# Selection scores of one block summed by ScalarE and GpSimd, its top-k rounds put last

## The chip, the cores and the metric

The kernel runs on 1 core of one Trainium2 chip. The metric is the time of one execution in microseconds (us), the median of several runs. The engines are TensorE (PE in the profile; its weight loads are PEld), VectorE (DVE), ScalarE (ACT), GpSimd (POOL) and SyncE (SP, which issues the transfers here). Each runs its own list of instructions in order and waits on the others by semaphores.

## The reference

A two-layer encoder for 512 frames of width 1024: layer one has sparse attention ("mixer A"), layer two latent attention, each followed by a squared-ReLU MLP. The change lies in mixer A, where a small indexer picks 128 keys for every query:

```python
logits = jnp.einsum('bthd,bsd->bths', qib, ki)          # 8 indexer heads
score = jnp.einsum('bths,bth->bts', jax.nn.relu(logits), wib)
score = jnp.where(visible[None], score, -jnp.inf)       # chunks of 64 frames
_, sel = lax.top_k(score, top_k)                        # top_k = 128
...
s = jnp.einsum('btgrd,btkgd->btgrk', qg, kg) * scale    # only the selected keys
p = jax.nn.softmax(s, axis=-1)
o = jnp.einsum('btgrk,btkgd->btgrd', p, vg)
```

The kernel doesn't gather keys: it makes a mask per query that is 0 for a selected key and a large negative number for the others, and adds it to all scores of the attention.

## The kernel before, in words

The 512 queries are four blocks of 128, numbered `qb` 0 to 3. Block 0 sees at most 128 keys, so it needs no selection. Block `qb` has `N = (qb + 1) * 128` key columns; "the second block" is `qb` 1 (256 columns), the third `qb` 2 (384), the fourth `qb` 3 (512).

Every product in float32 quality is made of three matmuls (`mm3`, L227 to L229) from a high and a low part of each operand. `Weights.convert` makes these parts: a cast on ACT (`w.._hi`, L143) and a subtraction on POOL (`w.._lo`, L150), five weight tiles ahead; a tile's buffer comes free when PE has used it.

In mixer A the order of the work is this:

- Projection of the indexer's rows (`ip`), with rotary embedding on DVE, the last for `inat[0]` (L390 to L393).
- `proj_tiles` is the projection of keys and values: 32 steps of three matmuls into the PSUM tiles `pp`, taken one at a time by `next(side)`, so that PE has work between other things.
- `q_turn` (L802) transposes the indexer's queries into `qip`, L811 its keys into `kip`; copies on ACT and differences on DVE give `qis` and `ki`.
- The score loop (L846): for each block and each of 8 heads one projection step, two matmuls `lp` (L852, L853; PSUM banks 0 and 1 in turn), for head 0 a relu and scaling on DVE (L856), for the others a relu on ACT (L859, tile `relu`) and `relu * weight + sum` on DVE (L860) into `acc[qb]`, which the trace calls `bias`.
- The selection, `rounds(qb)`: 16 rounds for each block, each a MAX8 (L829, the eight largest) and a MATCH_REPLACE8 (L831, which overwrites them with `TAKEN`; its first part shows as MATCH_VALUE_LOAD). Then L833 turns the block into its mask. `turns()` takes the blocks that are ready in rotation. Steps of it are drawn in the score loop and in the 64 steps of the query projection that follow (L927).
- Attention by head (`plan_heads`): scores `s_ps` on PE (L559), `top` on DVE, which adds the mask (L567; `smask` for block 0), exponential on ACT (L572), transposes (L578) and their parts, products with the values (L621), and the output projection `wo_ps` as a filler.

In the score loop PE's instructions keep the order in which they are written (`manual_schedule`), though later work may be put between them; a scheduler orders the other engines' lists, and PE's elsewhere, when the program is built. So a change in one place of mixer A gives new lists for all of it.

Of the kernel before, what the change touches and what calls it, by code (L numbers as in the profile page):

```python
# [11 lines left out]
F32 = mybir.dt.float32  # L12
F32R = mybir.dt.float32r
I32 = mybir.dt.int32
AF = mybir.ActivationFunctionType
OP = mybir.AluOpType
PSUM = bass.MemoryType.PSUM

P = 128
D = 1024  # L20
S = 512
NT = S // P
KD = D // P
CHUNK = 64
# [7 lines left out]
IDX_HEADS = 8  # L32
# [10 lines left out]

DFF = 4096
NEG = -1.0e30
FILL = -3.0e38
TAKEN = -3.4e38


RAWS = 3  # L50
# [154 lines left out]
def trunk(ctx: ExitStack, tc: tile.TileContext, x, positions, attn_norm, mlp_norm, a_w_in, a_w_out,  # L205
          b_w_in, b_q_norm, b_kv_norm, b_w_q_up, b_w_kv_up, b_w_out, mlp_w_up, mlp_w_down,
          final_norm, out):
    nc = tc.nc
# [17 lines left out]
    def mm3(ps, lh, ll, rh, rl, first, last):  # L226
        nc.tensor.matmul(ps, lh, rh, start=first, stop=False)  # L227
        nc.tensor.matmul(ps, lh, rl, start=False, stop=False)  # L228
        nc.tensor.matmul(ps, ll, rh, start=False, stop=last)  # L229
# [5 lines left out]

    lead = const.tile([P, 72], F32, name="lead")
    nc.gpsimd.memset(lead, 0.0)
    table = const.tile([P, 2], F32, name="table")
    nc.scalar.activation(table[:, 0:1], ones, AF.Sin)

# [271 lines left out]
    def run(gen):  # L512
        for _ in gen:
            pass
# [183 lines left out]
    def mixer_a():  # L698
        with ExitStack() as sa:
# [4 lines left out]
            bias = {qb: att.tile([P, (qb + 1) * P], F32, name=f"bias{qb}") for qb in range(1, NT)}  # L704
            with ExitStack() as sp:
                pr = sp.enter_context(tc.tile_pool(name="projA", bufs=1, reuse_waits="tile"))
# [47 lines left out]
                def proj_tiles(banks, done):  # L754

                    ps = [banks("pp") for _ in range(NT)]
                    for c in range(4):
                        wh, wl = W.take()[0]
                        for t in range(NT):
                            for i in range(2):  # L760
                                k = 2 * c + i
                                mm3(ps[t], hi[:, k, t * P:(t + 1) * P], lo[:, k, t * P:(t + 1) * P],
                                    wh[:, i, :], wl[:, i, :], k == 0, k == KD - 1)
                                if k == KD - 1:
                                    done(t, ps[t])
                                yield
# [18 lines left out]
                with tc.manual_schedule(engines={mybir.EngineType.PE}):  # L785
# [7 lines left out]
                            nc.vector.tensor_scalar(inat[t][:, 576:584], inat[t][:, 576:584], IDX_SCALE, None, op0=OP.mult)  # L793

                    side = proj_tiles(f_b, kv_done)
                    T_B, S_B = Banks(2, 3), Banks(0, 1)
                    qis, qps = [], {}

# [27 lines left out]
                    def rounds(qb):  # L826
                        for _ in range(TOPK // 8):
                            m8 = att.tile([P, 8], F32, name="m8", tag="m8", bufs=6)
                            nc.vector.max(m8, acc[qb])  # L829
                            yield  # L830
                            nc.vector.match_replace(out=acc[qb], in_to_replace=m8, in_values=acc[qb], imm_value=TAKEN)  # L831
                            yield
                        nc.vector.tensor_scalar(acc[qb], acc[qb], -3.2e38, NEG, op0=OP.is_gt, op1=OP.mult)  # L833

                    def turns():

                        while tops:
                            for g in list(tops):
                                if next(g, "end") == "end":
                                    tops.remove(g)  # L840
                                else:
                                    yield

                    acc, tops = bias, []
                    selection = turns()
                    for qb in range(NT - 1, 0, -1):  # L846
                        N = (qb + 1) * P
                        for h in range(IDX_HEADS):
                            next(side, None)
                            lp = S_B("lp")  # L850
                            q = qis[h][:, (qb - 1) * P:qb * P]
                            nc.tensor.matmul(lp[:, :N], q, ki1[:, :N], start=True, stop=False)  # L852
                            nc.tensor.matmul(lp[:, :N], q, ki2[:, :N], start=False, stop=True)  # L853
                            wcol = inat[qb][:, 576 + h:577 + h]
                            if h == 0:
                                nc.vector.tensor_scalar(acc[qb], lp[:, :N], 0.0, wcol, op0=OP.max, op1=OP.mult)  # L856
                            else:
                                r = pr.tile([P, 512], F32, name="relu", tag="relu", bufs=2)
                                nc.scalar.activation(r[:, :N], lp[:, :N], AF.Relu)  # L859
                                nc.vector.scalar_tensor_tensor(acc[qb], r[:, :N], wcol, acc[qb],  # L860
                                                               op0=OP.mult, op1=OP.add)
                            if tops:
                                next(selection, None)
                        nc.vector.memset(acc[qb][0:CHUNK, N - CHUNK:N], FILL)
                        tops.append(rounds(qb))
                    run(side)

            at = sa.enter_context(tc.tile_pool(name="attA2", bufs=1, reuse_waits="tile"))
# [397 lines left out]
```

## Time and profile before

| | us |
|---|---|
| runs | 1152.75, 1152.82, 1154.38 (median 1152.82) |
| the profiled execution | 1152.51 |
| its span, first to last instruction | 1150.7 |
| PE busy in the span | 1115.2 |
| DVE busy | 764.8 |
| mixer A's score loop, from its first `lp` | 51.42 |
| first `top` of a block that had a selection | 128.69 |

All times in the profile count from the start of the span. PE has work almost all the time, so what counts is where it stands, and for whom. A row of the timeline shows start, duration, engine, line, operation, output and inputs, the count, and in brackets the idle time before it with what ended it. "Window" rows show the window, its length, and for PE, PEld, DVE, ACT and POOL the busy time with the count, then PE's granted clock (1.00 is full), the share of the transfer engines, and GB/s.

### The profile page before, as it was taken

What the parts mean: (1) busy time and instruction counts of PE and PEld (TensorE: products, weight loads), DVE (VectorE), ACT (ScalarE), POOL (GpSimd) and SP (SyncE); (2) the same over time, 40 slices, a digit from 0 to 9 for tenths busy, and PEclk for the clock granted to TensorE, in tenths of its full rate; (3) what the DMA queues carried; (4) which work ended last, traced back from release to release, by engine and by line L of the source; (5) the groups of instructions that cost most, each with busy time, mean ns of one, the idle gap of its engine ahead of it and who ended that gap; (6) DMA issues with size and microseconds to landing.
All of it is one profiled execution on the core that took longest, in us unless ns stands there. A gap on an engine that the chain in (4) does not pass through costs nothing.

```text
span 1150.7 us, 15998 instructions
## 1 busy us (share of the span) xinstructions
PE 1115.2 (97%) x5725; PEld 948.2 (82%) x5725; DVE 764.8 (66%) x1420; ACT 608.8 (53%) x1119; POOL 661.7 (58%) x491
## 2 busy tenths in 40 slices
PE   8899889999999999999999999999999999999997
PEld 7778678879888888888889898787988888888886
DVE  6599998663566466466566788775556466556664
ACT  6453787644544554454445776563564454364452
POOL 5457433453657757856802543564557756866772
PEclk9999899999999999999999999999999999999999
DMA  6412100243124214313222201111524313412401
GB/s 203 119 55 92 56 1 2 74 140 99 62 85 146 90 57 147 125 57 112 71 77 79 76 15 42 56 56 56 172 63 132 128 52 113 147 56 91 147 15 77
DMA packets 65465, 99.04 MB, mean 86 GB/s; under 512 B 3173, under 2 KB 41833, under 8 KB 65386
## 3 DMA queue, kind: packets, MB, share of 16 engines
q1 hardware_dynamic: 65386, 98.03, 26.6%
q8 instruction: 45, 0.74, 0.3%
q14 instruction: 34, 0.28, 0.1%
HBM read 95.92 MB, written 2.10 MB: 85 GB/s over the span
## 4 chain that ended last, share of the span: by engine, by line
PE 83%; DVE 9%; ACT 3%; issue 3%; POOL 1%; DMA 0%; SPq 0%; DVEq 0%; POOLq 0%; ACTq 0%
PE dn L1196 22%; PE up L227 10%; PE up L228 10%; PE up L229 10%; PE s_ps L559 3%; PE o_ps L621 3%; PE pt_ps L578 3%; PE wo_ps L227 2%; PE wo_ps L228 2%; PE wo_ps L229 2%; DVE bias L831 2%; DVE m L829 2%; PE tps L453 1%; PE dn L228 1%; PE dn L227 1%
## 5 line engine op out<-in xcount | busy, mean ns | idle before, releaser
L148 POOL TENSOR_TENSOR w_lo<-quad,w_hi 128x512 fp32r<-128x512 f32 x196 | 275.7, 1438 | 161.7 <-ACT w_hi L143 159.3
L150 POOL TENSOR_TENSOR w_lo<-w_raw,w_hi 128x1024 fp32r<-128x1024 f32 (+4 forms) x117 | 265.6, 2289 | 92.1 <-ACT w_hi L143 89.9
L1199 DVE TENSOR_TENSOR x<-dn,x 128x512 f32<-128x512 f32 x196 | 134.9, 691 | 135.0 <-PE dn L1196 134.9
L228 PE MATMUL up<-hT_lo,w_hi 128*128 128x512 f32 (+1 forms) x576 | 210.5, 366 | 0.0
L227 PE MATMUL up<-hT_hi,w_hi 128*128 128x512 f32 (+1 forms) x576 | 209.4, 366 | 0.1
L229 PE MATMUL up<-hT_hi,w_lo 128*128 128x512 f32 (+1 forms) x576 | 208.5, 366 | 0.0
L143 ACT CAST w_hi<-w_raw 128x1024 fp32r<-128x1024 f32 (+6 forms) x112 | 111.7, 1006 | 153.9 <-PE dn L1196 55.1
L1196 PE MATMUL dn<-w_hi,lh 128*128 128x512 f32 x392 | 152.6, 389 | 0.3 <-DVE x L1199 0.3
L1196 PE MATMUL dn<-w_hi,ll 128*128 128x512 f32 x392 | 152.5, 389 | 0.0
L1196 PE MATMUL dn<-w_lo,lh 128*128 128x512 f32 x392 | 152.5, 389 | 0.0
L143 ACT CAST w_hi<-quad 128x1024 fp32r<-128x1024 f32 x98 | 101.0, 1050 | 95.3 <-DVE quad L86 74.6
L1161 DVE TENSOR_TENSOR ll<-u,lh 128x512 fp32r<-128x512 f32 x106 | 102.4, 996 | 41.3 <-ACT lh L1160 41.3
L229 PEld LDWEIGHTS up<-hT_hi,w_lo 128*128 128x128 f32 x576 | 108.7, 189 | 17.5
L228 PEld LDWEIGHTS up<-hT_lo,w_hi 128*128 128x128 f32 x576 | 108.6, 189 | 17.5 <-DVE hT_lo L458 0.2
L227 PEld LDWEIGHTS up<-hT_hi,w_hi 128*128 128x128 f32 x576 | 108.1, 189 | 17.7 <-ACT hT_hi L457 0.3
L86 DVE TENSOR_TENSOR quad<-quad 128x1024 f32<-128x1024 f32 x56 | 68.4, 1222 | 65.3 <-POOL w_lo L148 65.3
L1160 ACT CAST lh<-u 128x512 fp32r<-128x512 f32 x106 | 62.9, 620 | 78.4 <-DVE u L1173 70.4
L1196 PEld LDWEIGHTS dn<-w_hi,lh 128*128 128x128 f32 x392 | 73.6, 188 | 15.8 <-issue 0.7
L1196 PEld LDWEIGHTS dn<-w_hi,ll 128*128 128x128 f32 x392 | 73.6, 188 | 15.3
L1196 PEld LDWEIGHTS dn<-w_lo,lh 128*128 128x128 f32 x392 | 73.6, 188 | 15.3
L572 ACT ACTIVATE p<-p,m 128x128 f32<-128x128 f32 (+3 forms) x128 | 71.9, 563 | 17.8 <-DVE m L567 17.1
L591 ACT CAST pt_hi<-pt_ps 128x128 fp32r<-128x128 f32 (+3 forms) x128 | 52.9, 425 | 32.3 <-PE pt_ps L578 30.1
(230 smaller groups left out, 2233.9 us busy)
## 6 DMA issues: line engine op xcount, KB each, us to landing
w_raw<-in_mlp_w_up_dram SPq DMA_DIRECT2D x64, 512.0 KB, 3.7
quad<-in_mlp_w_down_dram SPq DMA_DIRECT2D x56, 512.0 KB, 3.6
w_raw<-in_a_w_in_dram SPq DMA_DIRECT2D x12, 512.0 KB, 3.6
w_raw<-in_a_w_out_dram SPq DMA_DIRECT2D x8, 512.0 KB, 3.2
w_raw<-in_mlp_w_down_dram SPq DMA_DIRECT2D x8, 512.0 KB, 4.2
w_raw<-in_b_w_out_dram SPq DMA_DIRECT2D x8, 512.0 KB, 3.7
x<-in_x_dram SPq DMA_DIRECT2D x4, 512.0 KB, 7.1
w_raw<-in_b_w_kv_up_dram SPq DMA_DIRECT2D x4, 512.0 KB, 3.8
```

Of the source, the lines that this page charges most:

```text
L86: self.nc.vector.tensor_sub(q[o], q[l], q[r])
L143: nc.scalar.copy(h, v)
L148: nc.gpsimd.tensor_sub(l[:, cs], v[:, cs], h[:, cs].bitcast(F32))
L150: (nc.gpsimd if engs[1] == "p" else nc.vector).tensor_sub(l, v, h.bitcast(F32))
L227: nc.tensor.matmul(ps, lh, rh, start=first, stop=False)
L228: nc.tensor.matmul(ps, lh, rl, start=False, stop=False)
L229: nc.tensor.matmul(ps, ll, rh, start=False, stop=last)
L572: nc.scalar.activation(U["p"][:, :N], U["p"][:, :N], AF.Exp, bias=U["m"], scale=-1.0, accum_out=pair["sums"][:, c:c + 1])
L1160: nc.scalar.copy(lh, v)
L1161: nc.vector.tensor_sub(ll, v, lh.bitcast(F32))
L1196: nc.tensor.matmul(pp[t], l[:, k, ts], r[:, k, :], start=first and k == 0 and m == 0, stop=k == 1 and m == 2, skip_group_check=True)
L1199: last = nc.vector.tensor_add(x[:, cs], pp[t], x[:, cs])
```

## The change

Six steps of the key and value projection are issued ahead of the indexer's transposes. The blocks' scores are made in the order fourth, second, third. The second block's heads 1 to 7 are scaled by their weight on ACT (a second ACTIVATE, L868 of the changed file) and added on POOL (L870), under a raised priority, and its visible edge is filled by POOL (L872). Its selection rounds don't start before the fourth block's have ended. There are four `relu` buffers in place of two. The masks are made by two dependent ACTIVATEs on ACT (L837, L838) in place of one TENSOR_SCALAR on DVE; for this `FILL` and `TAKEN` become powers of two with exact steps, and a constant column is set in `lead`.

```diff
-FILL = -3.0e38
-TAKEN = -3.4e38
+FILL = -1.5 * 2.0 ** 127
+TAKEN = -1.75 * 2.0 ** 127
...
+    nc.gpsimd.memset(lead[:, 64:65], -3.25)
...
                     side = proj_tiles(f_b, kv_done)
+                    for _ in range(6):
+                        next(side)
...
-                        nc.vector.tensor_scalar(acc[qb], acc[qb], -3.2e38, NEG, op0=OP.is_gt, op1=OP.mult)
+
+                        nc.scalar.activation(acc[qb], acc[qb], AF.Relu, bias=lead[:, 64:65], scale=-2.0 ** -126)
+                        nc.scalar.activation(acc[qb], acc[qb], AF.Copy, bias=-2.0 ** 100, scale=2.0 ** 102)
...
-                            for g in list(tops):
+                            for qb, g in list(tops):
+                                if qb == 1 and tops[0][0] == NT - 1:
+                                    continue
                                 if next(g, "end") == "end":
-                                    tops.remove(g)
+                                    tops.remove((qb, g))
...
-                    for qb in range(NT - 1, 0, -1):
+                    for qb in (3, 1, 2):
...
-                                r = pr.tile([P, 512], F32, name="relu", tag="relu", bufs=2)
+                                r = pr.tile([P, 512], F32, name="relu", tag="relu", bufs=4)
                                 nc.scalar.activation(r[:, :N], lp[:, :N], AF.Relu)
-                                nc.vector.scalar_tensor_tensor(acc[qb], r[:, :N], wcol, acc[qb],
-                                                               op0=OP.mult, op1=OP.add)
+                                if qb == 1:
+                                    nc.scalar.activation(r[:, :N], r[:, :N], AF.Copy, scale=wcol)
+                                    with tc.high_priority(400):
+                                        nc.gpsimd.tensor_add(acc[qb], acc[qb], r[:, :N])
+                                        if h == IDX_HEADS - 1:
+                                            nc.gpsimd.memset(acc[qb][0:CHUNK, N - CHUNK:N], FILL)
+                                else:
+                                    nc.vector.scalar_tensor_tensor(acc[qb], r[:, :N], wcol, acc[qb],
+                                                                   op0=OP.mult, op1=OP.add)
...
-                        nc.vector.memset(acc[qb][0:CHUNK, N - CHUNK:N], FILL)
-                        tops.append(rounds(qb))
+                        if qb != 1:
+                            nc.vector.memset(acc[qb][0:CHUNK, N - CHUNK:N], FILL)
+                        tops.append((qb, rounds(qb)))
```

What this does to the lists of instructions is shown at three places. The numbers in names tell tiles apart; `bias1` to `bias3` are the second to the fourth block, and line numbers after the change are those of the changed file (859 and 860 for the `lp` pair, 874 for DVE's sums).

First DVE, at the third block's seven sums (128x384). Before, they alternate with the fourth block's selection:

```order
L856 TENSOR_SCALAR bias2_125<-lp_724,inat2_134 128x384
L864 MEMSET bias3_126 64x64
L829 MAX m8_728<-bias3_126 128x8
L860 SCALAR_TENSOR_TENSOR bias2_125<-relu_736,inat2_134,bias2_125 128x384
L831 MATCH_REPLACE bias3_126<-m8_728,bias3_126 128x512
L860 SCALAR_TENSOR_TENSOR bias2_125<-relu_746,inat2_134,bias2_125 128x384
L829 MAX m8_749<-bias3_126 128x8
L860 SCALAR_TENSOR_TENSOR bias2_125<-relu_757,inat2_134,bias2_125 128x384
```

The same place on DVE after the change:

```order
L863 TENSOR_SCALAR bias2_126<-lp_883,inat2_135 128x384
L834 MATCH_REPLACE bias3_127<-m8_932,bias3_127 128x512
L832 MAX m8_963<-bias3_127 128x8
L834 MATCH_REPLACE bias3_127<-m8_963,bias3_127 128x512
L874 SCALAR_TENSOR_TENSOR bias2_126<-relu_892,inat2_135,bias2_126 128x384
L874 SCALAR_TENSOR_TENSOR bias2_126<-relu_899,inat2_135,bias2_126 128x384
L874 SCALAR_TENSOR_TENSOR bias2_126<-relu_907,inat2_135,bias2_126 128x384
L874 SCALAR_TENSOR_TENSOR bias2_126<-relu_914,inat2_135,bias2_126 128x384
L874 SCALAR_TENSOR_TENSOR bias2_126<-relu_922,inat2_135,bias2_126 128x384
L874 SCALAR_TENSOR_TENSOR bias2_126<-relu_929,inat2_135,bias2_126 128x384
L874 SCALAR_TENSOR_TENSOR bias2_126<-relu_937,inat2_135,bias2_126 128x384
L879 MEMSET bias2_126 64x64
```

The seven sums stand in one piece, and all further selection steps stand behind them.

Second PE, at two of the third block's score pairs. Before, one projection step (three matmuls) stands between two pairs:

```order
L852 MATMUL lp_733<-ki1_567,qis_587 128x384
L853 MATMUL lp_733<-ki2_568,qis_587 128x384
L227 MATMUL pp_543<-w8_hi_546,hT_hi_130 128x512
L228 MATMUL pp_543<-w8_lo_547,hT_hi_130 128x512
L229 MATMUL pp_543<-w8_hi_546,hT_lo_131 128x512
L852 MATMUL lp_743<-ki1_567,qis_597 128x384
L853 MATMUL lp_743<-ki2_568,qis_597 128x384
```

PE after the change, from the pair of the third block's head 5 to that of its last head (919, 926, 934; head 0 is 883):

```order
L859 MATMUL lp_919<-ki1_586,qis_644 128x384
L860 MATMUL lp_919<-ki2_587,qis_644 128x384
L228 MATMUL pp_1174<-w14_lo_955,hT_hi_131 128x512
L229 MATMUL pp_1174<-w14_hi_954,hT_lo_132 128x512
L228 MATMUL pp_1175<-w14_lo_955,hT_hi_131 128x512
L229 MATMUL pp_1175<-w14_hi_954,hT_lo_132 128x512
L227 MATMUL pp_1175<-w14_hi_954,hT_hi_131 128x512
...
L859 MATMUL lp_926<-ki1_586,qis_654 128x384
L860 MATMUL lp_926<-ki2_587,qis_654 128x384
L859 MATMUL lp_934<-ki1_586,qis_660 128x384
L860 MATMUL lp_934<-ki2_587,qis_660 128x384
```

Matmuls of the query projection, which is written later, have been put between the pairs: from head 0 to head 7 there are 10, 12, 8, 12, 4, 7 and 0 of them in the seven gaps, with four transposes of keys (kT) in the fifth. The last uses of weight tile w14 stand directly ahead of head 6's pair.

Third ACT and POOL, at the last relus of the third block after the change. ACT:

```order
L866 ACTIVATE relu_914<-lp_911 128x384
L866 ACTIVATE relu_922<-lp_919 128x384
L143 CAST w15_hi_1002<-w15_raw_674 128x1024
L866 ACTIVATE relu_929<-lp_926 128x384
L866 ACTIVATE relu_937<-lp_934 128x384
L899 CAST k1_1229<-kT_1204 64x512
```

POOL at the same place:

```order
L394 TENSOR_TENSOR knat_122<-rope_u_878,rope_v_879 128x4x16
L870 TENSOR_TENSOR bias1_125<-bias1_125,relu_851 128x256
L870 TENSOR_TENSOR bias1_125<-bias1_125,relu_863 128x256
L872 MEMSET bias1_125 64x64
L150 TENSOR_TENSOR w15_lo_1003<-w15_raw_674,w15_hi_1002 128x1024
L902 TENSOR_TENSOR k1_1229<-k1_1229,ones_67 64x512
```

The cast of weight tile w15, which takes the buffer of w14, has come to stand between the relus of heads 5 and 6, and its subtraction follows the second block's last sums on POOL; before, the cast of w13 stood at that place among the third block's relus.

## Prediction

> **What bounds the kernel now.** I read the page's busy times and chain first, then the windows, then who waits for whom.
>
> ```profile
> PE 1115.2 (97%) x5725; PEld 948.2 (82%) x5725; DVE 764.8 (66%) x1420; ACT 608.8 (53%) x1119; POOL 661.7 (58%) x491
> PE 83%; DVE 9%; ACT 3%; issue 3%; POOL 1%; DMA 0%; SPq 0%; DVEq 0%; POOLq 0%; ACTq 0%
> ...
> 38.00:64.00 26.00, 21.55 (x95) 17.06 (x93) 17.59 (x22) 12.90 (x23) 11.13 (x5) 0.93 0.32 86
> 64.00:129.00 65.00, 58.87 (x275) 48.74 (x275) 64.38 (x172) 29.28 (x51) 45.06 (x56) 0.99 0.24 80
> 129.00:250.00 121.00, 117.02 (x675) 98.51 (x676) 95.79 (x260) 85.43 (x229) 47.77 (x37) 0.98 0.10 32
> ...
> PE s_ps L559 <- DVE m L567: 6.3, 3, 5.5
> PE kip L811 <- DVE inat L393: 3.3, 1, 3.3
> ```
>
> TensorE (PE) is the bound everywhere but in one stage. In the window from 64 to 129 us VectorE (DVE, the third busy time) works 64.38 of 65 us and PE only 58.87: the selection sets the end there. PE loses 5.5 us where attention waits for the selection, and 3.3 us earlier at the key transposes (kip).
>
> ```profile
> 126.06 2.33 POOL L150 TENSOR_TENSOR w_lo<-w_raw,w_hi 128x1024 fp32r<-128x1024 f32 x1
> 126.27 2.27 DVE L833 TENSOR_SCALAR bias<-bias 128x256 f32<-128x256 f32 x1
> 128.69 0.42 DVE L567 CUSTOM_DVE_ANT_0 p<-s_ps,bias 128x256 f32<-128x256 f32 x1
> 129.17 1.54 PE L559 MATMUL s_ps<-k,qs 128*128 128x512 f32 x4 [5.52 <-DVE m L567]
> ```
>
> The second block's mask (L833) ends the selection, and the first instruction that reads it starts at 128.69. Whatever moves that instant moves the rest, since PE then has nothing else. So I work out when this instruction starts after the change.
>
> **PE up to the third block's scores.** The six projection steps (18 matmuls) now stand ahead of the transposes.
>
> ```profile
> 37.60 0.55 PE L802 MATMUL qip<-ident,inat 128*128 128x128 f32 x3
> 42.16 0.60 PE L811 MATMUL kip<-ident,inat 128*64 128x128 f32 x4 [3.33 <-DVE inat L393]
> 47.30 0.49 PE L802 MATMUL qip<-ident,inat 128*128 128x128 f32 x3
> 47.86 0.39 PE L228 MATMUL pp<-w_lo,hT_hi 128*128 128x512 f32 x1
> 49.57 0.39 PE L228 MATMUL pp<-w_lo,hT_hi 128*128 128x512 f32 x1
> 51.42 0.39 PE L852 MATMUL lp<-ki,qis 128*128 128x512 f32 x1
> 52.57 0.39 PE L852 MATMUL lp<-ki,qis 128*128 128x512 f32 x1
> 60.65 0.33 PE L852 MATMUL lp<-ki,qis 128*128 128x384 f32 x1
> 60.99 0.39 PE L227 MATMUL pp<-w_hi,hT_hi 128*128 128x512 f32 x1
> 75.09 0.28 PE L852 MATMUL lp<-ki,qis 128*128 128x256 f32 x1
> 76.02 0.28 PE L852 MATMUL lp<-ki,qis 128*128 128x256 f32 x1
> 89.05 0.39 PE L227 MATMUL pp<-w_hi,hT_hi 128*128 128x512 f32 x1
> 99.93 0.39 PE L227 MATMUL pp<-w_hi,hT_hi 128*128 128x512 f32 x1
> ```
>
> A projection matmul takes 0.23 us start to start (49.57 to 51.42 is eight; 89.05 to 99.93 is 48 at 0.227). From 37.60, 48 of them (11.1), four transpose groups at 0.33 (47.30 to 47.86 less one matmul) and kip (0.5) bring the first scores at 50.5, against 51.42: the 3.3 us wait and the slow matmuls after it go, but 18 matmuls more (4.1) stand ahead, so only 0.9 us is won. The kip input is no wait any more: it was there by 42.16 and is wanted at 42.9. Eight heads of the fourth block at 1.15 (51.42 to 52.57) reach 59.7; the second block's eight at 0.93 (75.09 to 76.02) end at 66.5; 22 projection matmuls later (5.0) the third block's first scores come at 71.5.
>
> Before, its eight pairs had three projection matmuls between them. Now, by the order, 10, 12, 8, 12, 4 (and the kT transposes), 7 and 0 stand between them: 53 x 0.227 = 12.0, seven pairs at 0.34 (60.65 to 60.99) 2.4, kT 0.5. The last pair starts at 86.4.
>
> **DVE.** It runs its list in order, and the third block's seven sums now stand in one piece, after nine selection rounds of the fourth block.
>
> ```profile
> 64.16 0.69 DVE L829 MAX8 m<-bias 128x8 f32<-128x512 f32 x1
> 65.95 0.61 DVE L860 SCALAR_TENSOR_TENSOR bias<-relu,inat,bias 128x384 f32<-128x384 f32 x1
> 89.77 1.47 DVE L829 MAX8 m<-bias 128x8 f32<-128x256 f32 x3
> 92.73 1.47 DVE L829 MAX8 m<-bias 128x8 f32<-128x256 f32 x3
> 119.44 0.88 DVE L829 MAX8 m<-bias 128x8 f32<-128x256 f32 x2
> 121.15 0.88 DVE L829 MAX8 m<-bias 128x8 f32<-128x256 f32 x2
> 124.30 0.43 DVE L829 MAX8 m<-bias 128x8 f32<-128x256 f32 x1
> 125.28 0.43 DVE L829 MAX8 m<-bias 128x8 f32<-128x256 f32 x1
> 129.63 0.69 DVE L907 TENSOR_TENSOR qs<-qT,qs 64x512 fp32r<-64x512 f32 x1
> 134.37 0.68 DVE L885 TENSOR_TENSOR k<-kT,k 64x512 fp32r<-64x512 f32 x1 [0.45 <-ACT k L884]
> ```
>
> A round of all three blocks takes 2.96 us (89.77 to 92.73), of the third and second 1.71 (119.44 to 121.15), so the fourth's share is 1.25. The second alone takes 0.98 (124.30 to 125.28) against a share by size of 0.68: a block alone loses 0.3 a round, since each step waits for the one before. The fourth's selection starts near 61.1 now (before: 64.16). Seven rounds alone (10.9), a MAX8, the third block's first head and three more steps (3.3) bring DVE to the seven sums at 75.3. There it must stand until PE's pairs come: the sums need 7 x 0.6 = 4.2 us, the matmuls between them hold them for over 11.
>
> ```profile
> 78.15 1.06 ACT L143 CAST w_hi<-w_raw 128x1024 fp32r<-128x1024 f32 x1
> 79.68 2.39 POOL L150 TENSOR_TENSOR w_lo<-w_raw,w_hi 128x1024 fp32r<-128x1024 f32 x1
> 79.96 2.40 DVE L860 SCALAR_TENSOR_TENSOR bias<-relu,inat,bias 128x256 f32<-128x256 f32 x1
> ```
>
> The end of the seven: w15's cast stands on ScalarE ahead of the sixth relu, and waits for w14's last matmul, directly ahead of the seventh pair, at 86.1. It ends at 87.3; GpSimd (POOL) then makes w15_lo until 89.7. The sixth sum becomes ready at 87.8, and meets it. In the rows above a sum of 256 columns took 2.40 us, ending as POOL's instruction ended, where even one of 384 takes 0.61 by itself; so I take 1.9 us for this wait (0 if they miss each other, 2.4 at most). The seven end at 90.9.
>
> What DVE then has left: seven rounds of the fourth (8.8), 16 of third and second (27.4), seven of the second alone at 0.25 extra (1.8; other work fills some gaps), four qs halves at 0.69 and two k halves at 0.68 (4.2, of which two qs and one k came after the masks before), 0.5 for the first head's small steps: 42.7. The end is 133.6.
>
> **The masks on ScalarE (ACT)**: two dependent instructions for each block in place of one on DVE.
>
> ```profile
> 77.67 0.74 POOL L777 TENSOR_TENSOR vva<-v,vva 128x256 fp32r<-128x256 f32 x1
> 77.88 0.38 ACT L859 ACTIVATE relu<-lp 128x256 f32<-128x256 f32 x1
> ```
>
> Two at 0.38 (bounds 0.3 and 0.6 each) and two hand-overs: 0.9 us on the path, against 2.27 on DVE, where L833 met POOL's subtraction. The third's and fourth's masks lie beside remaining rounds and cost nothing. The reader starts at 134.5: **128.69 + 5.8**.
>
> **The rest.** The second block's seven scalings (0.38) lie in ACT's idle 36 us of 64 to 129; its POOL sums are bounded by 0.74 (the same size) from below and 2.39 (four times the size, above) from above; I take 0.74. With POOL's key steps and w14_lo between them I estimate their end near 81, and DVE wants that block first after seven rounds of the pair (7 x 2.23), near 107: a cover of 25 us. What is queued behind them on POOL is w14_lo and the key ropes, wanted by PE from about 81: there the cover is some 6 us, and with sums at the upper bound it would be gone, at up to 1.65 x 4 = 7 us for the four ahead of w14_lo. Moved buffers, constants and the added memset: nothing. The DMAs up to there keep their order, and weights were converted ahead. The k half and two qs halves that are now done early give back between 0 and 2.0 us on DVE after the masks; I take 0, because PE sets that stage, at half clock:
>
> ```profile
> 128.00:133.00 5.00, 3.83 (x15) 3.45 (x16) 4.73 (x16) 3.32 (x10) 0.85 (x2) 0.50 0.34 105
> ```
>
> The same restart price recurs after the longer wait. The heads' order changes too; PE is busy 117 of 121 us there, so a gain is at most 1, a loss I bound by 4.
>
> Sum: 1152.51 (span 1150.7 with 1.8 around it) + 5.8 = 1158.3; the median of the runs, 1152.82, is 0.3 above the profiled one: **1158.5**. A change under 0.2% (2.3 us) can't be told from none here.
>
> **Rivals.** *Faster*: the matmuls between the pairs don't hold DVE. Against it stands the order: DVE can't pass a waiting sum. For it, DVE loses seven sums and three masks, and starts 3 us earlier. Its stand is 90.9 - 75.3 - 4.2 = 11.4; without it the reader starts at 123.1, 5.6 us earlier: 1147.2. It decides the sign where the stand falls under 5.6. [...] *About the same*: the sixth sum misses w15_lo (-1.9) and the early halves give back their 2.0: +1.9, 1154.7. *Slower still*: the reordered heads lose 4 more, as their waits fall on PE: 1162.5.
>
> **Chances**: as summed 0.64, slower still 0.10, about the same 0.12, faster 0.14. The range 1154 to 1163.5 leaves out the faster case and some of the tails, 0.2. Over 0.2% faster 0.14, within 0.11, slower 0.75.
>
> **What would show it.** No PE wait at kip; first scores near 50.5; the seven sums in a row on DVE with about 11 us idle before them, put down to ACT's relu, the last near 90; one sum of over 2 us beside POOL's w15_lo; the second block's mask on ACT near 133; PE waiting over 7 us there in place of 5.5. If DVE runs without idle time from 75 to 90, the forecast falls.

## The result, and the profile after

The changed kernel takes 1170.12 us (median of 4 runs, 1167.64 to 1170.54) against 1153.6 us for the kernel before, a ratio of 1.0137 with a 95% interval of 1.0118 to 1.0157. It is slower, as forecast, but by 16.5 us (14 to 18 by the interval) and not by 6; the time lies above the range. The profiled execution took 1170.54 us, 18.0 more than that of before.

| from start to start | before | after | difference |
|---|---|---|---|
| start of the span to the first `lp` | 51.4 | 51.3 | -0.1 |
| to the first masked `top` | 77.3 | 85.7 | +8.4 |
| to the first layer's first `up` matmul | 128.1 | 131.6 | +3.5 |
| to the second layer's first matmul (`bp`) | 328.3 | 329.4 | +1.1 |
| to the second layer's first `up` | 225.6 | 230.9 | +5.3 |
| to the last matmul's end | 333.3 | 333.3 | 0 |

Less than half of the loss lies where the change was made. The rest lies in stages whose code the change doesn't touch, more than half of that some 600 us later. First the page's busy times and its chain:

```profile
PE 1122.0 (96%) x5725; PEld 951.6 (81%) x5725; DVE 763.4 (65%) x1409; ACT 614.8 (53%) x1132; POOL 662.5 (57%) x500
PE 84%; DVE 7%; issue 3%; ACT 3%; POOL 2%; DMA 1%; SPq 0%; DVEq 0%; POOLq 0%; ACTq 0%
```

The same 5725 matmuls are busy for 6.8 us more (they last longer at the lower granted clock: one of 128x256 in `up` 0.41 us at 0.50, ahead of 271.3, and 0.28 at 1.00, behind it), and the span grows by 18.1, so PE also waits some 11 us longer. Two windows of mixer A, and PE's longest waits:

```profile
64.00:129.00 65.00, 55.80 (x249) 44.95 (x247) 54.20 (x140) 32.17 (x58) 46.65 (x64) 0.94 0.24 81
129.00:140.00 11.00, 3.55 (x14) 2.86 (x15) 8.47 (x29) 3.19 (x9) 2.03 (x2) 0.50 0.00 0
```

```profile
PE s_ps L560 <- DVE m L568: 7.6, 3, 6.8
PE s_ps L560 <- DVE qs L922: 5.7, 2, 5.5
PE tps L454 <- DVE h L426: 3.7, 1, 3.7
PE kT L893 <- DVE qs L922: 3.6, 1, 3.6
PE wo_ps L227 <- DVE x L531: 3.5, 5, 0.9
```

VectorE, which had worked 64.38 of the 65 us from 64 to 129, works 54.20 there: it stands for 10.8 us in the stage that it bounds. PE then waits three times for it (5.5, 3.6 and 6.8 us, at 117 to 137), where it had waited once (5.5). Two further waits belong to other stages: 3.7 us for `h` at the end of the first layer, and 3.5 us in five pieces for `x`, three of them in the second layer. Where VectorE stands, and how the selection ends:

```profile
76.58 0.83 DVE L874 SCALAR_TENSOR_TENSOR bias<-relu,inat,bias 128x384 f32<-128x384 f32 x1 [0.42 <-ACT relu L866]
79.68 0.62 DVE L874 SCALAR_TENSOR_TENSOR bias<-relu,inat,bias 128x384 f32<-128x384 f32 x1 [2.26 <-ACT relu L866]
81.80 0.62 DVE L874 SCALAR_TENSOR_TENSOR bias<-relu,inat,bias 128x384 f32<-128x384 f32 x1 [1.51 <-ACT relu L866]
84.95 0.62 DVE L874 SCALAR_TENSOR_TENSOR bias<-relu,inat,bias 128x384 f32<-128x384 f32 x1 [2.54 <-ACT relu L866]
86.67 0.62 DVE L874 SCALAR_TENSOR_TENSOR bias<-relu,inat,bias 128x384 f32<-128x384 f32 x1 [1.09 <-ACT relu L866]
87.84 0.35 PE L859 MATMUL lp<-ki,qis 128*128 128x384 f32 x1
88.82 2.39 POOL L150 TENSOR_TENSOR w_lo<-w_raw,w_hi 128x1024 fp32r<-128x1024 f32 x1 [9.22 <-ACT w_hi L143]
89.16 3.78 DVE L874 SCALAR_TENSOR_TENSOR bias<-relu,inat,bias 128x384 f32<-128x384 f32 x2 [1.88 <-ACT relu L866]
91.29 1.24 POOL L902 TENSOR_TENSOR k<-k,ones 64x512 fp32r<-64x512 f32 x1
...
135.56 0.41 DVE L834 MATCH_REPLACE8 bias<-m,bias 128x256 f32<-128x256 f32 x1
136.01 0.51 ACT L837 ACTIVATE bias<-bias,lead 128x256 f32<-128x256 f32 x1 [4.73 <-DVE bias L834]
136.55 0.42 ACT L838 ACTIVATE bias<-bias 128x256 f32<-128x256 f32 x1
137.00 0.42 DVE L568 CUSTOM_DVE_ANT_0 p<-s_ps,bias 128x256 f32<-128x256 f32 x1 [1.02 <-ACT bias L838]
```

The third block's seven sums wait 9.7 us in all for their relus (the brackets), which wait for PE's pairs. The last two take 3.78 us where two alone take 1.24: the sixth ends 0.4 us after w15_lo, the seventh 0.4 us after the key instruction that stands right behind it on POOL. Then VectorE works without a break, and the masks on ScalarE take 1.0 us.

At the end of the first layer PE's list differs, before first and then after:

```profile
252.55 1.03 PE L453 MATMUL tps<-ident,h 128*128 128x128 f32 x8
255.48 1.25 PE L453 MATMUL tps<-ident,h 128*128 128x128 f32 x8 [1.90 <-DVE hT_lo L458]
256.81 0.74 PE L227 MATMUL up<-hT_hi,w_hi 128*128 128x256 f32 x4
```

```profile
258.33 1.04 PE L454 MATMUL tps<-ident,h 128*128 128x128 f32 x8
261.82 0.50 PE L227 MATMUL wo_ps<-w_hi,oh 128*128 128x512 f32 x1 [0.87 <-DVE x L531]
267.21 1.75 PE L454 MATMUL tps<-ident,h 128*128 128x128 f32 x8 [3.73 <-DVE h L426]
268.61 0.99 PE L227 MATMUL up<-hT_hi,w_hi 128*128 128x256 f32 x3
```

Before, eight transposes of `h` follow all output matmuls (`wo_ps`), and the next eight wait 1.90 us. After, six such matmuls, a wait of 0.87 and six more follow the first eight transposes; the output matmuls end later against them, and the next transposes wait 3.73. These two waits are 2.7 us longer than the one before, most of the 3.5 that the stage loses. The second layer, again before and then after:

```profile
740.00:760.00 20.00, 16.67 (x110) 14.73 (x109) 12.39 (x35) 10.96 (x31) 13.50 (x8) 1.00 0.17 54
```

```profile
755.00:775.00 20.00, 16.68 (x92) 14.99 (x91) 10.87 (x32) 9.38 (x25) 13.16 (x8) 0.83 0.18 53
```

```profile
748.50 0.35 PE L227 MATMUL vp<-w_hi,ck_hi 128*128 128x256 f32 x1 [1.54 <-DVE qn L415]
791.01 0.50 PE L227 MATMUL wo_ps<-w_hi,oh 128*128 128x512 f32 x1 [0.33 <-DVE x L530]
```

```profile
761.29 0.36 PE L227 MATMUL vp<-w_hi,ck_hi 128*128 128x256 f32 x1 [1.53 <-DVE qn L416]
801.94 0.50 PE L227 MATMUL wo_ps<-w_hi,oh 128*128 128x512 f32 x1 [0.78 <-DVE x L531]
810.71 0.50 PE L227 MATMUL wo_ps<-w_hi,oh 128*128 128x512 f32 x1 [0.78 <-DVE x L531]
```

The wait ahead of the values (`vp`) is as long as before (1.53 against 1.54), but here the granted clock falls to half behind it (0.83 in the mean of 20 us, 0.50 from 762.82 to 769.65). Then three output matmuls wait 0.78 each for `x` (the first and the last are shown), where one waited 0.33 before.

### The profile page after: what moved, and what is told of

Read it like the earlier page. It is cut to its first block, busy times and chain, and to the rows that moved or that the text cites. A ratio compares the mean times of both kernels' runs of the same rounds, so it can differ in the third digit from the quotient of the medians.

```text
span 1168.8 us, 16004 instructions
## 1 busy us (share of the span) xinstructions
PE 1122.0 (96%) x5725; PEld 951.6 (81%) x5725; DVE 763.4 (65%) x1409; ACT 614.8 (53%) x1132; POOL 662.5 (57%) x500
## 4 chain that ended last, share of the span: by engine, by line
PE 84%; DVE 7%; issue 3%; ACT 3%; POOL 2%; DMA 1%; SPq 0%; DVEq 0%; POOLq 0%; ACTq 0%
PE dn L1211 22%; PE up L227 10%; PE up L228 10%; PE up L229 10%; PE o_ps L622 3%; PE s_ps L560 3%; PE pt_ps L579 2%; PE wo_ps L227 2%; PE wo_ps L228 2%; PE wo_ps L229 2%; DVE bias L834 2%; DVE m L832 1%; PE tps L454 1%; PE dn L228 1%; PE dn L229 1%
## 5 line engine op out<-in xcount | busy, mean ns | idle before, releaser
L573 ACT ACTIVATE p<-p,m 128x128 f32<-128x128 f32 (+3 forms) x128 | 72.1, 564 | 18.1 <-DVE m L568 17.6
```

Source lines behind the costliest of these rows:

```text
L573: nc.scalar.activation(U["p"][:, :N], U["p"][:, :N], AF.Exp, bias=U["m"], scale=-1.0, accum_out=pair["sums"][:, c:c + 1])
```

## The experiments

Theory A: the matmuls between the third block's pairs hold VectorE's list, and that alone makes the selection end late. Theory C: the remaining 9.9 us come from the lists that the scheduler made anew for the end of the first layer and for the second layer. The rivals: the second block's late rounds alone make the selection late (B); the later stages are late only because the selection was (D). "Half clock" below is the time at a granted clock of 0.5 around `vp`.

| kernel | first masked top | to first `up` | second layer | half clock | median us | ratio to before (95%) |
|---|---|---|---|---|---|---|
| before, profiled | 128.69 | 128.1 | 225.6 | 0 | 1152.82 | |
| after | 137.00 | 131.6 | 230.9 | 6.8 | 1170.12 | 1.0137 (1.0118 to 1.0157) |
| x1_masks | 128.51 | 132.2 | 230.9 | 6.8 | 1161.19 | 1.0063 (1.0048 to 1.0078) |
| x2_nosteps | 125.13 | 131.7 | 227.1 | 3.4 | 1154.88 | 1.0014 (1.0003 to 1.0025) |
| x3_pin | 133.53 | 131.7 | 227.5 | 6.8 | 1162.06 | 1.0070 (1.0055 to 1.0085) |
| x4_nopool | 138.66 | 132.8 | 225.9 | 0 | 1168.02 | 1.0122 (1.0107 to 1.0137) |
| y1_steps | 135.93 | 128.5 | 228.3 | 6.8 | 1160.63 | 1.0060 (1.0039 to 1.0081) |
| y2_bpin | 127.69 | 132.7 | 228.1 | 6.8 | 1157.20 | 1.0032 (1.0015 to 1.0048) |
| y3_321_dvemask | 123.72 | 131.5 | 225.5 | 0 | 1153.22 | 0.9991 (0.9974 to 1.0007) |
| y4_321 | 122.47 | 129.4 | 228.9 | 0 | 1152.49 | 0.9985 (0.9974 to 0.9997) |
| z1_321_five | 125.01 | 130.2 | 228.2 | 6.8 | 1151.79 | 0.9982 (0.9969 to 0.9995) |
| z2_seven | 137.33 | 128.5 | 227.0 | 3.4 | 1162.64 | 1.0079 (1.0061 to 1.0098) |
| z3_nomasks | 137.79 | 131.6 | 229.8 | 3.4 | 1169.57 | 1.0154 (1.0125 to 1.0184) |
| z4_last_mask | 129.00 | 130.2 | 225.8 | 0 | 1155.62 | 1.0013 (1.0003 to 1.0022) |

The stages are those of each profiled execution, the medians those of all runs of a kernel, in whose executions the half clock need not fall alike. 1152.82 is the median of the first three executions of the kernel before; the ratios use those that ran beside each kernel (medians 1153.6 to 1154.3).

### The hold of VectorE's list

**x2_nosteps**, the changed kernel with one edit:

```diff
-                    for _ in range(6):
-                        next(side)
```

> The changed kernel without the six projection steps ahead of the transposes; 3 projection matmuls stand between the third block's pairs again (19 in the sixth gap, 1 in the last). Theory A (matmuls between the pairs hold VectorE, and that alone made the selection end late): the seven sums end near 83 in place of 92.94, with less than 3 us of idle time before them, 41.8 us of work follow (43.0 less one round) and ScalarE's masks take 1.0: the first masked top at 125 to 127. Rival B (the second block's rounds, alone at the end, make it late whatever PE does): 133 or later. Total by A: 1149 to 1153, if the second layer's order (here a third one) costs 0 to 3; by B 1159 or more.

```profile
80.00 3.26 DVE L872 SCALAR_TENSOR_TENSOR bias<-relu,inat,bias 128x384 f32<-128x384 f32 x2
125.13 0.43 DVE L568 CUSTOM_DVE_ANT_0 p<-s_ps,bias 128x256 f32<-128x256 f32 x1
```

No bracket stands at these sums: VectorE never waited for a relu there. The seven end at 83.26, the first masked top starts at 125.13, 11.9 us earlier than in the changed kernel and 3.6 earlier than before. That is theory A; the second block's rounds still come last here, so B falls. Yet the first `up` comes at 256.8, as before: the 3.6 us are lost again in the next stage, and the median (1154.88) lies above the 1149 to 1153 expected.

**x4_nopool**, the changed kernel with the second block's sums back on VectorE:

```diff
-                                if qb == 1:
+                                if qb == 9:
                                     nc.scalar.activation(r[:, :N], r[:, :N], AF.Copy, scale=wcol)
...
-                        if qb != 1:
+                        if True:
                             nc.vector.memset(acc[qb][0:CHUNK, N - CHUNK:N], FILL)
```

> The changed kernel with the second block's sums on VectorE again (no scaling on ScalarE, no sums on GpSimd); the gaps between the third block's pairs hold 20, 0, 22, 0, 20, 0, 17 matmuls, 79 in all. Theory A (the hold sets the end; what VectorE is relieved of before it is worth nothing): the seven sums of the third block end within 1.5 us of 92.9, and the first masked top starts at 136 to 138, as in the changed kernel. Rival B (the sums moved to GpSimd do relieve VectorE): the seven sums' 3.5 us come on top, 140 or later. Total by A 1165 to 1170, and by B 1169 to 1174; the second layer has a third order here.

From its first `lp` (53.7) the masked top comes 85.0 us later, against 85.7 in the changed kernel. So relieving VectorE of seven sums was worth nothing there, as theory A has it: the last pair comes 36.0 us after the first `lp` (36.5 in the changed kernel), and they lie inside the time for which VectorE is held anyway. The absolute values missed by 0.4 and 0.7 because the first `lp` comes 2.4 us late.

**x3_pin**, the changed kernel with the first half of the query projection inside the stretch in which PE's order is kept:

```diff
                     run(side)
+                    n = 0
+                    for _ in proj_tiles(Banks(0, 1, 6, 7), lambda t, ps: q_done(0, t, ps)):
+                        n += 1
+                        next(selection, None)
+                        if n % 2:
+                            next(selection, None)
...
-            n = 0
-            for i in range(2):
+            for i in (1,):
```

> The changed kernel with the first half of the query projection written inside the stretch in which PE's order is kept; the gaps between the third block's pairs then hold 3, 4, 0, 0, 8, 12, 0 (27 in all, with the last matmuls 31) in place of 57 matmuls, and the six steps stay ahead. Theory A (the hold): the last pair starts near 81, the seven sums end near 82.5, 42.4 us of work follow, 1.0 for the masks: first masked top at 125 to 127, 1149 to 1153 with the second layer's order as in the run without the steps. Rival B (the second block's rounds alone): 133 or later, 1159 or more.

The top came at 133.53, where the rival had it, and not at 125 to 127; the median is the rival's too. But the seven sums ended at 91.17 and not at 82.5, and the rows show a hold of another kind:

```profile
40.81 2.42 DVE L393 TENSOR_TENSOR rope_u<-inat,ropeC_a 128x16 f32<-128x16 f32 x1
43.27 2.28 DVE L394 TENSOR_TENSOR inat<-rope_u,rope_v 128x16 f32<-128x16 f32 x1
...
73.79 2.37 POOL L150 TENSOR_TENSOR w_lo<-w_raw,w_hi 128x1024 fp32r<-128x1024 f32 x1
75.02 5.08 DVE L874 SCALAR_TENSOR_TENSOR bias<-relu,inat,bias 128x384 f32<-128x384 f32 x1 [0.42 <-ACT relu L866]
79.59 0.69 POOL L394 TENSOR_TENSOR knat<-rope_u,rope_v 128x64 f32<-128x64 f32 x1
80.74 0.44 PE L859 MATMUL lp<-ki,qis 128*128 128x384 f32 x1 [2.42 <-ACT relu L866]
```

The first sum met POOL in an unbroken run of instructions (the first and the last of the ten that it overlaps stand above) and took 5.08 us in place of 0.62; the four `relu` buffers stayed full, and PE's next pair waited for it. The last two rope instructions took 2.42 and 2.28 us (0.16 and 2.26 in the changed kernel), so that the keys came some 2.5 us later. So this run doesn't tell A from B by itself: it put a wait beside POOL in place of the hold. From the sums' end to the last round VectorE took 41.3 us here, 40.6 in x2_nosteps and 43.0 in the changed kernel; when the sums end differs more, 83.26 to 92.94.

**y1_steps**, the kernel before with only the six steps:

```diff
                     side = proj_tiles(f_b, kv_done)
+                    for _ in range(6):
+                        next(side)
```

> The kernel before with the six projection steps ahead of the transposes as the only edit. The block scored last (here the second, summed on VectorE) has 19, 1, 24, 0, 20, 0, 15 = 79 matmuls in its gaps, and six of its sums in one piece on VectorE. Theory A (matmuls between the pairs hold VectorE's list): the last of these sums ends near 89.5, about 41.3 us of selection work are left then, and the first masked top starts at 130 to 133 although VectorE's selection begins some 3 us earlier. Rival B (no hold): 128.69 less 3, 125.6. The end of the first layer and the second layer have PE's order of the kernel before, so by the theory that these orders cost time in the changed kernel, the first 'up' comes 128.1 +- 1 after the masked top here, and the second layer takes 225.6 +- 0.5 from its first projection to its first 'up'. By A 1154 to 1157, by B 1149 to 1151.

```profile
90.06 3.62 DVE L862 SCALAR_TENSOR_TENSOR bias<-relu,inat,bias 128x256 f32<-128x256 f32 x2 [3.12 <-ACT relu L861]
135.93 0.42 DVE L567 CUSTOM_DVE_ANT_0 p<-s_ps,bias 128x256 f32<-128x256 f32 x1
263.07 1.26 PE L453 MATMUL tps<-ident,h 128*128 128x128 f32 x8 [1.90 <-DVE hT_lo L458]
```

The six steps alone move the masked top by 7.2 us, without the new order of blocks, POOL's sums or the masks: issued early, they are missing between the last block's pairs, where the query projection is put in heaps instead. The last two sums met POOL here too (3.62 us where the two ahead of them take 1.07, beside POOL's 2.40 from 89.82 and 1.10 from 92.29; they end at 93.7 and not at 89.5), hence the miss upward. The second layer missed too: 228.3 where 225.6 was expected, with the half clock.

### The lists of the later stages

**x1_masks**, the kernel before with the masks on ScalarE (and the constants that they need):

```diff
-                        nc.vector.tensor_scalar(acc[qb], acc[qb], -3.2e38, NEG, op0=OP.is_gt, op1=OP.mult)
+                        nc.scalar.activation(acc[qb], acc[qb], AF.Relu, bias=lead[:, 64:65], scale=-2.0 ** -126)
+                        nc.scalar.activation(acc[qb], acc[qb], AF.Copy, bias=-2.0 ** 100, scale=2.0 ** 102)
```

> The kernel before with the three masks on ScalarE as the only edit. VectorE's list up to the masks stays as before, so the first masked top moves only by what the masks cost: three VectorE masks (0.34 to 0.41 us, and 2.27 where the last met GpSimd) go, 1.03 us of ScalarE comes, one qs half (0.69) stands ahead: 127.5 +- 0.7 in place of 128.69. The list of the second layer's attention, though, is the one that the changed kernel has. Theory A (the order of the second layer costs time by itself): the first 'up' comes 0 to 1.5 us early, yet from there to the end the kernel loses about 5 us as the changed kernel did (2.2 for its waits for x, about 3 if the clock falls to half at the second layer's values): 1154 to 1158. Rival B (the second layer lost time because it came later): nothing is lost there, 1151.5.

The masks moved the masked top by 0.2 us, less than the 1.2 expected, and the kernel lost 7.6 us all the same: the first `up` comes 132.2 after the top (128.1 before), the second layer takes 230.9, as in the changed kernel. An expectation of 1154 to 1158 had left out the end of the first layer, whose list had changed here too.

**y2_bpin**, the kernel before with the edit of x3_pin and nothing else; it has the changed kernel's list at the end of the first layer, and the second layer's list of before:

> The kernel before, with the first half of the query projection written inside the stretch in which PE's order is kept; nothing else. The selection stays as it is: first masked top at 127.5 to 129.5. PE's order at the end of the first layer becomes that of the changed kernel (eight transposes of h ahead of the last 18 output matmuls), the second layer keeps that of the kernel before. Theory C (that order costs 3.6 us by itself): first 'up' 131.7 +- 0.7 after the masked top, near 260.5, second layer 225.6 (or up to 3 more where the clock falls to half at its values): 1155.5 to 1159. Rival D (the end of the first layer came late because of the selection's tail): 128.1 after the masked top, 1151.5 to 1153.5.

```profile
127.69 0.42 DVE L567 CUSTOM_DVE_ANT_0 p<-s_ps,bias 128x256 f32<-128x256 f32 x1
258.73 1.81 PE L453 MATMUL tps<-ident,h 128*128 128x128 f32 x8 [3.74 <-DVE h L425]
260.36 1.01 PE L227 MATMUL up<-hT_hi,w_hi 128*128 128x256 f32 x3
```

The selection ended 1.0 earlier than before, and the first `up` came 3.6 later, with the changed kernel's wait of 3.7 us: theory C for this stage. (Twelve output matmuls stand behind the first eight transposes, not the 18 expected.) **z2_seven** goes the other way, from the changed kernel:

```diff
-                    for _ in range(6):
+                    for _ in range(7):
```

> The changed kernel with seven projection steps ahead of the transposes in place of six, nothing else. The hold stays (19, 4, 16, 4, 11, 0, 4 matmuls at the third block's pairs, its seven sums in one piece), while the lists for the first layer's end and for the second layer become those of the kernel before. Theory C (those lists cost 3.5 + 1 and about 2.5 us): first masked top at 136 to 139, first 'up' 128 to 129 after it, second layer 225.6, or 228.2 with the half clock at its values: 1161 to 1166. Rival D (these stages were late because the selection was): 131 to 132 and 230.9, 1169 to 1173.

```profile
137.33 0.42 DVE L568 CUSTOM_DVE_ANT_0 p<-s_ps,bias 128x256 f32<-128x256 f32 x1 [1.02 <-ACT bias L838]
264.48 1.26 PE L454 MATMUL tps<-ident,h 128*128 128x128 f32 x8 [1.90 <-DVE hT_lo L459]
265.81 0.73 PE L227 MATMUL up<-hT_hi,w_hi 128*128 128x256 f32 x4
```

With the selection as late as in the changed kernel, the first `up` comes 128.5 after it, the next stage takes 328.3, the second layer 227.0, and the median falls by 7.5 us to 1162.64. D falls. Over all 14 kernels of the table the stage to the first `up` takes 128.1 to 130.2 where these transposes wait 1.90 us, and 131.5 to 132.8 where they wait 3.7.

For the second layer, seven kernels have the list of before. Without the half clock it takes 225.6 (before), 225.5 (y3) and 225.8 (z4), with 3.4 us of it 227.0 (z2), with 6.8 us 228.3 (y1), 228.1 (y2) and 228.2 (z1). So a half clock of 6.8 us costs 2.6 there. The changed kernel's 230.9, less such an amount, leaves some 2.7 us for its list, in which the waits for `x` are 2.0 longer than before. So the lists account for some 6.2 of the 9.9 us (3.5 and 2.7), and theory C overstates them: 2.6 is a half clock that the list of before shows as well, in four of its seven kernels. The 1.1 in the stage between goes with a half clock too, in the first 2.7 us behind the first `up` (268.6 to 271.3 in the changed kernel); all eight kernels that wait 3.7 ahead of it have one there, and one of the other six.

### The order of the blocks, and a faster version

**y3_321_dvemask** and **y4_321** are the changed kernel with the old order of blocks, the first also with the old masks:

```diff
-                    for qb in (3, 1, 2):
+                    for qb in (3, 2, 1):
```

> The changed kernel with the blocks in the order fourth, third, second, and the masks on VectorE as before. The matmuls stand between the second block's pairs now (19, 1, 24, 0, 20, 0, 15), whose sums run on GpSimd, so VectorE has no sum behind them. Theory A (the hold, through VectorE's list, is what cost the time): VectorE works without a stand from 61 on and the first masked top starts at 119 to 123; first 'up' 131.7 later (order of the first layer's end as in the changed kernel), second layer as in the kernel before: 1145 to 1149. Rival B (the second block alone at the end, 12 rounds at 0.98, makes it late): 128 or later, and 1155 or more.

> The changed kernel with the blocks in the order fourth, third, second; masks on ScalarE. Theory A: VectorE without a stand, first masked top at 119.5 to 123.5. The orders of the first layer's end and of the second layer are new ones here (neither that of the kernel before nor of the changed one): if orders matter, first 'up' comes 128 to 133 after the top and the second layer takes 225.5 to 231, so 1144 to 1153; Rival B as in the run with masks on VectorE: top at 128 or later, 1155 or more.

The same matmuls as in y1_steps stand between the last block's pairs (60, four of them transposes; the expectations' 79 count 19 that stand ahead of its first pair), but its sums run on GpSimd, and VectorE has nothing waiting for them: the top comes at 123.72 and 122.47, about 14 us earlier than in the changed kernel. This is theory A from the other side, and POOL's sums are worth their price in this order (y1_steps, without them, without the four buffers and without the later rounds, had 135.93). y3 still missed its total, 1153.22 against 1145 to 1149. What is won at the masked top (5.0 and 6.2 us) is partly given back: y3 in the end of the first layer (131.5), y4 in the second layer (228.9, with the three waits of 0.78 and no half clock). **z1_321_five** takes five steps in place of six:

> The changed kernel with the blocks in the order fourth, third, second, and five projection steps ahead of the transposes in place of six. The one step fewer gives the lists of the kernel before for the first layer's end and for the second layer. Theory A + C (the hold of VectorE's list, and the orders behind it, are the whole loss): first masked top at 121 to 124, first 'up' 128 to 129 after it, second layer 225.6, or 228.2 where the clock falls to half at its values: 1146 to 1150, faster than both kernels. Rival (with orders as before, something else in the second block's late rounds costs PE time): first 'up' over 130 after the top, 1151 or more.

It has both later lists of the kernel before, and its first `up` waits 1.90. Its median is 1151.79: a little faster than before, and 1.6% faster than the changed kernel, but slower than the 1146 to 1150 expected. The first `up` came 130.2 us after the top, over 130 as its rival had it, and 2.1 more than before with the same list at that stage's end. In the profiled execution the granted clock was half from 117.2 to 130.9, 13.7 us against 6.8 in y4_321 and before (in the mean of the span it was 0.987, against 0.996 and 0.995). That cause is not tested by an edit. And the masked top itself came late:

```profile
122.36 0.51 ACT L837 ACTIVATE bias<-bias,lead 128x256 f32<-128x256 f32 x1 [0.39 <-DVE bias L834]
122.89 1.28 ACT L573 ACT_TABLE_LOAD   x1
124.58 0.40 ACT L838 ACTIVATE bias<-bias 128x256 f32<-128x256 f32 x1
```

Between the two mask instructions ScalarE's list has a table load and an exponential of the first block, which has no selection: 1.7 us. **z4_last_mask** therefore puts this one mask back on VectorE:

```diff
+                        if qb == 1:
+                            nc.vector.tensor_scalar(acc[qb], acc[qb], -1.625 * 2.0 ** 127, NEG, op0=OP.is_gt, op1=OP.mult)
+                        else:
```

> The version with the old order of blocks and five steps, with the last mask alone (second block) on VectorE. In that version's trace ScalarE had a table load (1.28) and an exponential (0.59) between the two mask instructions, and the first masked top came 1.76 us after VectorE was free. Theory A: that wait goes and 0.35 comes: top at 123.2 to 124.2 in place of 125.01, about 1.3 us less in all, 1149.5 to 1151.5 (the first layer's end gets the list of the run at 129.4, the second layer keeps that of the kernel before). Rival: the top comes as early, but PE waits for the keys and queries (qs) there, and nothing is won: 1151.5 to 1153.

It lost instead, 1155.62:

```profile
39.43 2.43 DVE L393 TENSOR_TENSOR rope_u<-inat,ropeC_a 128x16 f32<-128x16 f32 x1
41.89 2.27 DVE L394 TENSOR_TENSOR inat<-rope_u,rope_v 128x16 f32<-128x16 f32 x1
126.61 2.25 DVE L838 TENSOR_SCALAR bias<-bias 128x256 f32<-128x256 f32 x1
```

The mask took 2.25 us, as in the kernel before (2.27, beside POOL's subtraction of 126.06 to 128.39) and against 0.29 in y1_steps; that it met POOL here too is the author's reading of that length. The two rope instructions both met POOL (2.43 and 2.27 us, beside its three subtractions from 37.06 to 44.12), where in z1_321_five the first took 0.16: the first `lp` came 3.3 us later, with the same edit elsewhere. Neither theory had that. z1_321_five stays the fastest version tried, and the three of this order with ratios under 1 can't be told apart.

**z3_nomasks**, the changed kernel with the masks on VectorE, all else in the lists alike:

> The changed kernel with the masks on VectorE again; every other list stays as in the changed kernel. Theory A: three VectorE masks of about 0.35 to 0.4 us come (GpSimd is idle where the last one stands), ScalarE's 1.03 goes: the first masked top at 136.6 to 137.4, total within 1 us of the changed kernel, 1169 to 1171. Rival B (the masks on ScalarE are what made it late): 135 or earlier, 1168 or less.

The top comes at 137.79, 0.4 above the expectation and 0.8 later than with ScalarE's masks: the masks on ScalarE are at most a small gain at that place, and not a part of the loss there. The medians (1169.57 and 1170.12) can't be told apart; one of the four executions took 1177.46, and nothing on record shows why.

## Why the prediction was wrong

The direction and the mechanism at the selection were right, the size was not: 1158.5 forecast, 1170.12 measured.

- **First scores**: no wait at kip, as forecast, and the first scores at 51.3 (50.5 forecast). x3_pin and z4_last_mask show that this hung on one rope instruction: the last but one took 2.42 and 2.43 us there, and 0.16 in the changed kernel.
- **The third block's pairs**: first at 72.8 (71.5), last at 87.8 (86.4).
- **The seven sums**: in a row, waiting for ScalarE's relus, as described; 9.7 us idle and 2.5 beside POOL, 12.2 in all (11.4 forecast). They end at 92.94 (90.9). The forecast let one sum meet POOL; the next met the key instruction that followed.
- **VectorE's remaining work**: 43.0 us (42.7). **Masks**: 1.03 from the last round to the reader (0.9).
- **The reader**: 137.0, so +8.3 where the sum said +5.8.
- **POOL's sums**: 0.74 us each (0.736 to 0.755), done at 79.6 (near 81), with no effect on the end, as forecast.
- **The rest: 0.** This is the step that failed: 9.9 us of the 18.0 between the profiled executions. The reader's 2.5 us more are the rest of the miss. The prediction looked at the attention's heads ("a gain is at most 1, a loss I bound by 4"), not at the lists behind them. The end of the first layer cost 3.5, the clock behind it 1.1, and the second layer 5.3 (some 2.7 by its list, 2.6 by the half clock); the lists and the clock behind mixer A had neither a term nor a rival. Whether the half clock falls at `vp` is not set by that layer's list: that of before shows it with 0, 3.4 and 6.8 us. The lists themselves were there as soon as the program was built. PE's waits in the profile of before (1.9 us at `tps`, 1.5 at `vp`, 0.3 at `wo_ps`) were where to price them.
- **The same restart price recurs**: this held. The clock stayed at half for 20.5 us around the longer waits, against 6.8 before, but 15.9 of them lay ahead of the reader, and 4.6 behind it against 6.1 before. z2_seven and y1_steps, with the list of before at that stage's end, need 128.5 us from the top to the first `up`, 0.4 more than before.
- **Rivals**: "slower still" (1162.5) came nearest, but put its loss on the heads. "Faster" is what happens without the hold (125.13 in x2_nosteps, 123.1 in the rival), and there too the later lists took the gain.

## What to carry to other kernels

Filler work spent early is missing later: count what is left to put between the pairs of the last block, and look what an in-order engine has queued behind the sums that wait for them. Where a scheduler makes the lists, an edit in one stage can reorder stages that it doesn't touch, so compare the lists to the program's end and price every wait of the old profile whose neighbours moved. A change of 0.2% should be tried with two or three neutral variants (one step more or fewer) before it is judged.

## What the runs showed of the hardware

A VectorE instruction lasted longer beside several GpSimd instructions: in x3_pin a sum took 5.08 us, from 75.02 to 80.10 (0.62 in the changed kernel at 79.68, with POOL idle), beside ten POOL instructions that follow each other without a gap. The longest of the ten takes 2.37 us, so the sum outlasted every one of them.

The granted clock fell to half around `vp` in nine of the fourteen profiled executions and not in the five others (the table). In the changed kernel PE waits 0.73, 0.23, 1.53 and 0.83 us there, within 8 us, and the clock is 0.50 from 762.82 to 769.65; in the kernel before PE waits 0.73, 0.23, 1.54 and 0.83, and the clock stays at 1.00. z2_seven and z3_nomasks, where it fell, and z4_last_mask, where it did not, have the same waits to 0.01 us. Each wait is far shorter than the shortest stretch at half clock of these two traces, 3.41 us; up to PE's last matmul the times between two changes of the clock are multiples of it in both (at half clock 20.48, 3.41 and 6.83 us after, 3.41 and 6.83 before). Laid on steps of this length, PE's idle time in the step just ahead of the fall is 2.00 us (759.41 to 762.82), and in the kernel before no step around `vp` holds more than 1.54 (745.82 to 749.23). No run here set where the waits lie in these steps, so what decides is not shown.
